# One-hot gate rows by two 1024-column fp16 vector operations per four tokens

## Chip, core and metric

The kernel runs on one core of one Trainium2 chip. The metric is the device time of the whole program in microseconds (us). The core's engines work side by side, each through its own queue in order: TensorE (PE in the profile; its weight loads are listed apart as PEld), VectorE (DVE), ScalarE (ACT), GpSimd (POOL) and SyncE (SP, which only issues transfers here).

## What is computed

One inference step of a decoder layer for 256 prompt tokens and 32 sample tokens: a norm, one input projection, a gated convolution branch, a windowed attention branch, their gated sum, and then PEER, a retrieval over 128 x 128 experts of one neuron each. The change touches only PEER, and there only the prompt tokens:

```python
def body(hc):
    qh = (hc @ wq).reshape(PEER_CHUNK, PEER_HEADS, 2, PEER_HALF)
    s1 = jnp.einsum('chd,hnd->chn', qh[:, :, 0], k1)
    s2 = jnp.einsum('chd,hnd->chn', qh[:, :, 1], k2)
    v1, i1 = lax.top_k(s1, PEER_TOPK)
    v2, i2 = lax.top_k(s2, PEER_TOPK)
    ...
    sv, si = lax.top_k(cand, PEER_TOPK)
    eidx = jnp.take_along_axis(cidx, si, axis=-1)
    gate = jax.nn.softmax(sv, axis=-1)
    act = jax.nn.gelu(jnp.einsum('cd,chkd->chk', hc, u_tab[eidx]))
    return jnp.einsum('chk,chkd->cd', gate * act, v_tab[eidx])
```

Each prompt token picks 8 heads x 16 experts, so 128 pairs (i1, i2) with a gate each. The kernel does not gather for the prompt: it multiplies the tokens with all 16384 rows of `u`, weights the result with a dense table of gates that is zero where no expert was picked, and multiplies that with all rows of `v`.

## The kernel before

Weights come in blocks of 128 x 1024 f32 (368 of them, 512 KB each). Every block is split by `split_next` into a rounded part `whi` (ScalarE, line 106) and the remainder `wlo` (VectorE, line 107, or GpSimd for the blocks in `pool_lo`), three blocks ahead of their use, and each product is three passes (lines 125 to 127).

The part of PEER that the change is about is the loop `for i in range(128)` (line 1025), one iteration for each of the 128 blocks of `u`:

- While the top-k of the tokens is not finished, an iteration does a piece of that on VectorE (`topk_some`). When it is finished the temporary pool `tk` is closed, `act1` is opened, and `gates()` begins (line 1032).
- From then on an iteration issues, in this order: `place_new` for gate tiles that are complete (ScalarE), the split of the block two ahead, the multiplication left over from the iteration before (`late`, line 959, VectorE), `place_held` (line 980, VectorE), one step of `gates()` through `gate_some` (now and then two steps, so that the 67 steps end at block 124), and `run_s(i)`: 24 matmuls of 256 columns, then the GELU by ScalarE, in one piece (line 961) for tokens without gates so far and through the tile `ev` (line 958) for tokens that have them.
- A step of `gates()` takes a group `u` of GT = 4 tokens. `hot(u + 2)` makes, two steps ahead, the one-hot rows on VectorE; then TensorE multiplies the rows of group `u` (line 1008, 8 matmuls of 128 columns) into half of a `wide` tile of 8 tokens, which `place_new` and `place_held` read later. 256 tokens are 64 groups.
- `hot(u)`, lines 985 to 994: the 128 picks of a token lie on the 128 partitions. For each token one operation compares a row 0..127 (`iotaR`, fp16) with the pick's i2 (line 990, tile `hot`, 128 columns), and two more compare with i1 and multiply with the gate's fp16 high and low part (line 992, tile `wgt`). That is 12 operations of 128 columns for a group. The indices and gates are per-partition scalars in f32, from `idxT` and `gaT`, which lines 883 to 891 write when the top-k of 128 tokens is finished.
- The rows `hot` are the weights that TensorE loads, the rows `wgt` are streamed.

VectorE takes its operations in the order in which they are issued; so does TensorE. After the loop comes the product with `v` (line 1079).

Of the kernel before, what the change touches and what calls it, by code (L numbers as in the profile page):

```python
# [10 lines left out]
F32 = mybir.dt.float32  # L11
F32R = mybir.dt.float32r
F16 = mybir.dt.float16
# [3 lines left out]
OP = mybir.AluOpType  # L17
AX = mybir.AxisListType

P = 128  # L20
D = 1024
NT = 288
NP = 256
# [17 lines left out]
GT = 4  # L41
# [24 lines left out]
def emit(ctx, tc, a):  # L66
    nc = tc.nc
    V, S, T, G, SY = nc.vector, nc.scalar, nc.tensor, nc.gpsimd, nc.sync
# [50 lines left out]
    def weights(b):  # L119
        split_ahead(b)  # L120
        return halves.pop(b)
# [88 lines left out]
    with ExitStack() as ca:  # L210
        pa = ca.enter_context(tc.tile_pool(name="pa", bufs=1, side="right"))
        with ExitStack() as c1:
# [78 lines left out]
            def proj(b):  # L291
                w = weights(b)
                xH, xL = xin[0]
                clk[0] = b
                o = acc.get()
                for k in range(KT):
                    if k == KT // 2:
                        flow.step()
                    s = slice(k * P, (k + 1) * P)
                    if b:  # L300
                        mm3(o[:, :NT], (w[0][:, s], w[1][:, s]), (xH[:, k, :], xL[:, k, :]), k == 0, k == KT - 1)
                        continue
                    T.matmul(o[:, :NT], w[0][:, s], xH[:, k, :], start=k == 0, stop=False)
                    T.matmul(o[:, :NT], w[0][:, s], xL[:, k, :], start=False, stop=False)
                for k in range(0 if b else KT):
                    s = slice(k * P, (k + 1) * P)
                    T.matmul(o[:, :NT], w[1][:, s], xH[:, k, :], start=False, stop=k == KT - 1)
                return o[:, :NT]
# [197 lines left out]
            for t in range(3):  # L506
                w = P if t < 2 else NS
# [15 lines left out]
            for i in range(12):  # L523
                o = proj(B_Q + i)
                if i == 0:
                    b = bg.get()
                    for t in range(3):
                        w = P if t < 2 else NS
# [124 lines left out]
            for c in range(8):  # L653
                flow.step()
                w = weights(B_AG + 2 * c)
                clk[0] = B_AG + 2 * c
                o = acc.get()
# [9 lines left out]
                e = wk.tile([P, NT], F32, tag="t", name=f"ga{c}", bufs=5)  # L667
# [36 lines left out]
            for c in range(0, 8, 2):  # L704
                flow.step()
                w = weights(B_BG + 5 * (c // 2))
                ybs = []
                for f in range(2):
                    o = acc.get()
# [7 lines left out]
                for f in range(2):  # L717
                    flow.step()
                    gp = proj(B_BG + 5 * (c // 2) + 1 + 2 * f)
                    e = wk.tile([P, NT], F32, tag="t", name=f"gb{c}_{f}", bufs=5)  # L720
# [61 lines left out]
    kp = ctx.enter_context(tc.tile_pool(name="kp", bufs=1))  # L782
# [2 lines left out]
        S.dma_start(h2rep[32 * q:32 * q + 32, :], h2d)  # L785
    eidx = kp.tile([P, 32], I32, name="eidx")
    gateS = kp.tile([P, 32], F32, name="gateS")
    idxT = kp.tile([P, 2, NP], F32, name="idxT")
    gaT = kp.tile([P, 2, NP], F32, name="gaT")
    iotaR = kp.tile([P, P], F16, name="iotaR")  # L790
    G.dma_start(iotaR, a["iotaR"])
    coh = ExitStack()
    oh = coh.enter_context(tc.tile_pool(name="oh", bufs=1))

    ra = ctx.enter_context(ExitStack())
    pact0 = ra.enter_context(tc.tile_pool(name="pact0", bufs=1, side="right"))
# [2 lines left out]
    tk = ct.enter_context(tc.tile_pool(name="tk", bufs=1, side="right"))  # L799
# [75 lines left out]
    def topk_all():  # L875
        for t in range(2):
            r = [tk.tile([P, 8, TOPK], F32, tag=f"r{i}", name=f"r{t}_{i}", bufs=1) for i in range(3)]
            yield from topk(scores[t], 8, f"tp{t}", r, lambda h: 2 * h + 2 <= scored[0])
            b = bg.get()
            for i in range(3):  # L880
                T.transpose(b[:, i * P:(i + 1) * P], r[i].rearrange("p h k -> p (h k)"), ident)
            yield 0.1
            tt = slice(t * P, (t + 1) * P)
            V.tensor_copy(idxT[:, :, tt], b[:, 0:2 * P].rearrange("p (f c) -> p f c", f=2))
            gs = tk.tile([P, P], F32, tag="gs", name=f"gs{t}", bufs=1)
            V.tensor_scalar_mul(gs, b[:, 2 * P:3 * P], GSCALE)
            bg.put()
            g16 = tk.tile([P, P], F16, tag="g16", name=f"g16_{t}", bufs=1)
            V.tensor_copy(g16, gs)
            V.tensor_copy(gaT[:, 0, tt], g16)  # L890
            V.tensor_sub(gaT[:, 1, tt], gs, g16)
            yield 0.8
        s = tk.tile([P, 16, P], F32, tag="s", name="s_smp", bufs=2)
        b = bg.get()
        for jf in range(4):
            for q in range(4):
                T.matmul(b[32 * q:32 * q + 32, jf * P:(jf + 1) * P], qh[:, 4 * q + jf, NP:NT], keys[:, 4 * q + jf, :],
                         start=True, stop=True, tile_position=(0, 32 * q))
        V.tensor_copy(s[:, 0:4, :].rearrange("p a b -> p (a b)"), b)
        bg.put()  # L900
        yield 1.0
        i1s = tk.tile([P, 2, TOPK], F32, name="i1s")
        i2s = tk.tile([P, 2, TOPK], F32, name="i2s")
        yield from topk(s, 2, "ts", (i1s, i2s, gateS.rearrange("p (h k) -> p h k", h=2)), lambda h: True)
        V.scalar_tensor_tensor(i1s, i1s, 128.0, i2s, op0=OP.mult, op1=OP.add)
        V.tensor_copy(eidx.rearrange("p (h k) -> p h k", h=2), i1s)
        yield 0.3
# [4 lines left out]
    def topk_some(x):  # L912
        budget[0] = min(budget[0], 1.0) + x
        while budget[0] > 0 and not done[0]:
            r = next(gen, 0)
            if r == 0:
                done[0] = True
            elif r is None:
                return
            else:  # L920
                budget[0] -= r
# [11 lines left out]
    for j in range(16):  # L933
        w = weights(B_WQ + j)
        o = acc.get()
# [29 lines left out]
    def place_new(u, full):  # L965
        tt = slice(u * 8, u * 8 + 8)
        f = full.rearrange("p (t i) -> p i t", t=8)
        for c in range(2):
            n = min(max(held[0] - 64 * c, 0), 64)
            if n < 64:  # L970
                S.activation(act[c][:, n:, tt], f[:, 64 * c + n:64 * c + 64, :], AF.Copy, scale=1.0 / GSCALE)
# [11 lines left out]

    def gates():
        def hot(u):
            e = oh.tile([P, GT, P], F16, tag="hot", name=f"hot{u}", bufs=3)
            w = oh.tile([P, GT, 2, P], F16, tag="wgt", name=f"wgt{u}", bufs=3)
            for j in range(GT):
                t = u * GT + j
                V.tensor_scalar(e[:, j, :], iotaR, idxT[:, 1, t:t + 1], None, op0=OP.is_equal)  # L990
                for i in range(2):
                    V.tensor_scalar(w[:, j, i, :], iotaR, idxT[:, 0, t:t + 1], gaT[:, i, t:t + 1],  # L992
                                    op0=OP.is_equal, op1=OP.mult)
            return e, w

        n = NP // GT
        made = {}
        for u in range(-2, n):
            if u + 2 < n:
                made[u + 2] = hot(u + 2)  # L1000
            if u >= 0:
                if u % 2 == 0:
                    full = wide.get()
                e, w = made.pop(u)
                for j in range(GT):
                    jj = (u % 2) * GT + j
                    for i in range(2):
                        T.matmul(full[:, jj * P:(jj + 1) * P], e[:, j, :], w[:, j, i, :], start=i == 0, stop=i == 1)
                if u % 2:
                    placing.append((u // 2, full))  # L1010
            yield
        yield

    placing = []
    gg, first = None, [None]

    def gate_some(i):
        n = 3 + NP // GT
        while stepped[0] < min(n, (i - first[0]) * n / (124 - first[0])):
            assert next(gg, 1) is None  # L1020
            stepped[0] += 1
# [3 lines left out]
    for i in range(128):  # L1025
        if not done[0]:
            topk_some(1.6 if i % 2 else 2.4)
        elif gg is None:
            ct.close()
            pact1 = ra.enter_context(tc.tile_pool(name="pact1", bufs=1, side="right"))  # L1030
            act[1] = pact1.tile([P, 64, NP], F32, name="act1")
            gg, first[0] = gates(), i
        for x in placing:
            place_new(*x)
        split_ahead(B_U + i)
        for f in late:
            f()
        late.clear()
        for x in placing:
            place_held(*x)  # L1040
        placing.clear()
        if gg is not None:
            gate_some(i)
        run_s(i)
        copy_some(1 if i % 4 == 0 else 0)
# [73 lines left out]
    for i in range(V_END):  # L1119
# [14 lines left out]
        if i == 121:  # L1134
            for n in range(2):
                b = bg.get()
# [46 lines left out]
def host(inp):  # L1183
    f = {k: np.ascontiguousarray(np.asarray(v)) for k, v in inp.items()}
    d = {}
# [25 lines left out]
    for g, nm in enumerate(("cache_kv_w128", "cache_kv_w512", "cache_kv_w2048")):  # L1211
        c = f[nm][0]
        d[f"cache{g}"] = c.reshape(8, c.shape[1], D)
        if g == 2:
            c = c[:, rows2]
# [13 lines left out]
    con[:, 160:176] = np.arange(16, dtype=np.float32)[None]  # L1229
    con[:, 176] = EPS  # L1230
    d["consts"] = con
    d["iotaR"] = np.ascontiguousarray(np.broadcast_to(np.arange(P)[None, :], (P, P))).astype(np.float16)

    def dist_mask(dq, win, dil):
        ok = (dq >= 0) & (dq <= win) & (dq % dil == 0)
# [2 lines left out]
    q = np.arange(P)[:, None]  # L1238
# [6 lines left out]
    b4, sl, tt = (x.reshape(-1)[:, None] for x in np.meshgrid(np.arange(4), np.arange(8), np.arange(4), indexing="ij"))  # L1245
# [48 lines left out]
```

## Time and profile before

| | us |
|---|---|
| median of three runs (1338.0 to 1339.51) | 1339.17 |
| the profiled execution: its own time | 1339.22 |
| the profiled execution: span from first to last instruction | 1337.4 |
| TensorE busy in the span | 1277.6 |
| VectorE busy in the span | 1009.7 |
| ScalarE busy in the span | 585.5 |

The page of the profile gives busy time by engine and by slices of the span, the chain of work that ended last, and the groups of instructions by line. The trace behind it can be asked for stretches of time: busy time of each engine in a window, the instructions of one engine in order of time, and groups by line in a window. In an ordered list a row has the start in us, the duration in us, the engine, the line, the operation, what it writes and reads, and the count of instructions merged into it; in brackets stands the idle time of the engine before it and what the profile names as its end. Durations of successive instructions of one engine overlap, because they are pipelined: what an instruction costs in a row of others is the distance from its start to the next start.

### The profile page before, as it was taken

The page shows a single profiled execution, that of the slowest core. Times are in us where ns is not written, and L with a number is a line of the kernel's source. Part 1 is how long each engine was busy: PE and PEld are TensorE (multiplying, and loading weights), DVE is VectorE, ACT ScalarE, POOL GpSimd, SP SyncE. Part 2 cuts the span into 40 slices and gives each one's busy share as a digit, 9 for nine tenths or more (in the row PEclk, how much of TensorE's full clock was granted, in tenths as well). Part 3 has the DMA queues.
Part 4 walks back from the last instruction along what each step waited for, and adds up shares of the span by engine and source line. Part 5 has one row for each costly group of instructions (what it writes and reads, how often), then busy time and mean ns, then how long its engine had stood idle before and what let it go on. Part 6 is the DMA issues. An engine that isn't in the chain of part 4 may idle for free.

```text
span 1337.4 us, 23676 instructions
## 1 busy us (share of the span) xinstructions
PE 1277.6 (96%) x9132; PEld 1140.0 (85%) x9132; DVE 1009.7 (75%) x2348; ACT 585.5 (44%) x971; POOL 182.2 (14%) x122
## 2 busy tenths in 40 slices
PE   6999999999999899999999998999999999999995
PEld 6998998888998899899998887888888888888873
DVE  5736276673593458999989999999868878787874
ACT  4334443433462445445344333333445555555542
POOL 4000000000250133444000000000001111111100
PEclk7999999999999899999999998999999999999998
DMA  7586766655586678677765555555678888888874
GB/s 279 193 314 256 245 236 229 226 207 205 166 258 218 237 250 285 235 270 265 265 232 198 189 189 174 189 189 178 219 283 297 308 297 308 306 303 291 314 277 145
DMA packets 68065, 325.15 MB, mean 243 GB/s; under 512 B 8576, under 2 KB 8736, under 8 KB 59120
## 3 DMA queue, kind: packets, MB, share of 16 engines
q1 hardware_dynamic: 55744, 249.46, 53.6%
q0 software_dynamic: 9760, 67.15, 13.1%
q10 hardware_dynamic: 2448, 7.03, 1.5%
q8 instruction: 72, 1.18, 0.4%
q14 instruction: 41, 0.34, 0.1%
HBM read 317.50 MB, written 60.24 MB: 282 GB/s over the span
## 4 chain that ended last, share of the span: by engine, by line
PE 68%; DVE 25%; DMA 3%; ACT 2%; issue 2%; SPq 0%; DVEq 0%; ACTq 0%; POOLq 0%
PE wide L1079 24%; PE acc L125 12%; PE acc L126 11%; PE acc L127 11%; DVE wgt L992 8%; DVE wlo L107 7%; DVE hot L990 3%; PE bg L760 3%; DVE act L980 2%; DMA raw<-wpack 2%; PE bg L380 1%; PE bg L349 1%; PE bg L468 1%; PE bg L414 1%; ACT whi L106 1%
## 5 line engine op out<-in xcount | busy, mean ns | idle before, releaser
L107 DVE TENSOR_TENSOR wlo<-raw,whi 128x1024 fp32r<-128x1024 f32 x327 | 406.4, 1244 | 223.7 <-ACT whi L106 222.2
L106 ACT CAST whi<-raw 128x1024 fp32r<-128x1024 f32 x360 | 378.1, 1050 | 193.2 <-PE wide L1079 158.3
L125 PE MATMUL acc<-h2H,whi 128*128 128x256 f32 (+1 forms) x1152 | 331.9, 288 | 0.0
L127 PE MATMUL acc<-h2H,wlo 128*128 128x256 f32 (+1 forms) x1152 | 327.3, 284 | 4.3 <-DVE wlo L107 4.0
L126 PE MATMUL acc<-h2L,whi 128*128 128x256 f32 (+1 forms) x1152 | 329.3, 286 | 0.1
L125 PEld LDWEIGHTS acc<-h2H,whi 128*128 128x128 f32 x1152 | 220.0, 191 | 11.3 <-ACT act L961 5.5
L127 PEld LDWEIGHTS acc<-h2H,wlo 128*128 128x128 f32 x1152 | 218.0, 189 | 4.9 <-DVE wlo L107 4.4
L126 PEld LDWEIGHTS acc<-h2L,whi 128*128 128x128 f32 x1152 | 219.5, 190 | 0.4 <-DVE h2L L191 0.4
L125 PE MATMUL acc<-hH,whi 128*128 128x288 f32 x512 | 157.7, 308 | 3.3 <-ACT yb L714 2.4
L1079 PE MATMUL wide<-whi,ah 128*128 128x512 f32 x504 | 155.5, 390 | 1.6 <-ACT ah L1066 1.6
L1079 PE MATMUL wide<-whi,al 128*128 128x512 f32 x504 | 155.2, 389 | 0.0
L1079 PE MATMUL wide<-wlo,ah 128*128 128x512 f32 x504 | 155.2, 389 | 0.0
L127 PE MATMUL acc<-hH,wlo 128*128 128x288 f32 x512 | 150.8, 294 | 1.0 <-DVE wlo L107 1.0
L126 PE MATMUL acc<-hL,whi 128*128 128x288 f32 x512 | 151.1, 295 | 0.0
L992 DVE TENSOR_SCALAR wgt<-iotaR,idxT,gaT 128x128 f16<-128x128 f16 x512 | 133.5, 298 | 0.0
L1079 PEld LDWEIGHTS wide<-whi,ah 128*128 128x128 f32 x504 | 94.4, 188 | 22.2 <-ACT ah L1066 2.7
L1079 PEld LDWEIGHTS wide<-wlo,ah 128*128 128x128 f32 x504 | 94.6, 188 | 19.7
L1079 PEld LDWEIGHTS wide<-whi,al 128*128 128x128 f32 x504 | 94.6, 188 | 19.6
L125 PEld LDWEIGHTS acc<-hH,whi 128*128 128x128 f32 x512 | 96.0, 188 | 15.6 <-issue 8.5
L107 POOL TENSOR_TENSOR wlo<-raw,whi 128x1024 fp32r<-128x1024 f32 x33 | 84.1, 2550 | 121.8 <-ACT whi L106 121.8
L127 PEld LDWEIGHTS acc<-hH,wlo 128*128 128x128 f32 x512 | 96.3, 188 | 1.2 <-DVE wlo L107 1.2
L126 PEld LDWEIGHTS acc<-hL,whi 128*128 128x128 f32 x512 | 96.3, 188 | 0.0
(317 smaller groups left out, 1630.6 us busy)
## 6 DMA issues: line engine op xcount, KB each, us to landing
raw<-wpack SPq DMA_DIRECT2D x368, 512.0 KB
kvs<-cache SPq DMA_DIRECT2D x32, 1020.0 KB
kvs<-cache SPq DMA_DIRECT2D x16, 1016.0 KB
kv<-kc POOLq DMA_DIRECT2D x14, 1024.0 KB, 7.3
kv<-vc POOLq DMA_DIRECT2D x14, 1024.0 KB, 6.1
kvs<-cache SPq DMA_DIRECT2D x8, 496.0 KB
kT_out<-kT ACTq DMA_DIRECT2D x1, 1728.0 KB
v_out<-vn ACTq DMA_DIRECT2D x6, 256.0 KB
```

The lines of the kernel that those rows point to most:

```text
L106: S.copy(hi, raw)
L107: (G if i in pool_lo else V).tensor_sub(lo, raw, hi.bitcast(F32))
L125: T.matmul(out, wh, xh, start=first, stop=False)
L126: T.matmul(out, wh, xl, start=False, stop=False)
L127: T.matmul(out, wl, xh, start=False, stop=last)
L349: T.matmul(dst, qT[rows, g * 4 + pr, t * P:(t + 1) * P], kT[rows, g * 4 + pr, 0:w], start=True, stop=True)
L380: T.matmul(o[rows, :P], vn[:, kb, g * 512 + s * HD:g * 512 + (s + 1) * HD], pt[:, j, :], start=j == 0, stop=j == nb - 1)
L760: T.matmul(o, x, wo[k][m][:, nn], start=k == 0 and i == 0, stop=k == KT - 1 and i == 2)
L980: V.scalar_tensor_tensor(sl, f[:, 64 * c:64 * c + n, :], 1.0 / GSCALE, sl, op0=OP.mult, op1=OP.mult)
L990: V.tensor_scalar(e[:, j, :], iotaR, idxT[:, 1, t:t + 1], None, op0=OP.is_equal)
L992: V.tensor_scalar(w[:, j, i, :], iotaR, idxT[:, 0, t:t + 1], gaT[:, i, t:t + 1], op0=OP.is_equal, op1=OP.mult)
L1079: T.matmul(vacc[t][:, nn], x[:, tt], w[:, nn], start=i == 0 and j == 0, stop=i == 127 and j == 2)
```

## The change

`hot(u)` makes the rows of a group with two operations in place of twelve. Both tiles become 1024 columns of fp16. The first operation (`tensor_tensor`, is_equal) compares `iotaR` with both indices of the four tokens at once; its tile holds the one-hot rows of i1 (f = 0) and of i2 (f = 1). The second (`tensor_tensor`, mult) multiplies the rows of i1 with the high and with the low part of the gate; it reads what the first wrote. Indices and gates are no longer scalars but columns that are repeated 128 times. Tokens are interleaved in pairs, so that the innermost run of each operand is two neighbouring fp16 elements, one of each token; `iotaR` holds each number twice for this. The matmuls therefore read every second column of the tiles, for the weights and for the streamed rows. `idxT` and `gaT` become fp16 and are laid out by groups; the separate copy `g16` is gone. The pool `oh` (tiles `hot`, `wgt`, `ev`) is opened where `gates()` begins, and no longer before the top-k.

```diff
--- before.py
+++ after.py
@@ -785,12 +785,10 @@
         S.dma_start(h2rep[32 * q:32 * q + 32, :], h2d)
     eidx = kp.tile([P, 32], I32, name="eidx")
     gateS = kp.tile([P, 32], F32, name="gateS")
-    idxT = kp.tile([P, 2, NP], F32, name="idxT")
-    gaT = kp.tile([P, 2, NP], F32, name="gaT")
-    iotaR = kp.tile([P, P], F16, name="iotaR")
-    G.dma_start(iotaR, a["iotaR"])
-    coh = ExitStack()
-    oh = coh.enter_context(tc.tile_pool(name="oh", bufs=1))
+    idxT = kp.tile([P, NP // GT, 2, GT], F16, name="idxT")
+    gaT = kp.tile([P, NP // GT, 2, GT], F16, name="gaT")
+    iotaR = kp.tile([P, P, 2], F16, name="iotaR")
+    G.dma_start(iotaR.rearrange("p a b -> p (a b)"), a["iotaR"])
 
     ra = ctx.enter_context(ExitStack())
     pact0 = ra.enter_context(tc.tile_pool(name="pact0", bufs=1, side="right"))
@@ -880,15 +878,14 @@
             for i in range(3):
                 T.transpose(b[:, i * P:(i + 1) * P], r[i].rearrange("p h k -> p (h k)"), ident)
             yield 0.1
-            tt = slice(t * P, (t + 1) * P)
-            V.tensor_copy(idxT[:, :, tt], b[:, 0:2 * P].rearrange("p (f c) -> p f c", f=2))
+            uu = slice(t * P // GT, (t + 1) * P // GT)
+            V.tensor_copy(idxT[:, uu], b[:, 0:2 * P].rearrange("p (f u c) -> p u f c", f=2, c=GT))
             gs = tk.tile([P, P], F32, tag="gs", name=f"gs{t}", bufs=1)
             V.tensor_scalar_mul(gs, b[:, 2 * P:3 * P], GSCALE)
             bg.put()
-            g16 = tk.tile([P, P], F16, tag="g16", name=f"g16_{t}", bufs=1)
-            V.tensor_copy(g16, gs)
-            V.tensor_copy(gaT[:, 0, tt], g16)
-            V.tensor_sub(gaT[:, 1, tt], gs, g16)
+            gs = gs.rearrange("p (u c) -> p u c", c=GT)
+            V.tensor_copy(gaT[:, uu, 0, :], gs)
+            V.tensor_sub(gaT[:, uu, 1, :], gs, gaT[:, uu, 0, :])
             yield 0.8
         s = tk.tile([P, 16, P], F32, tag="s", name="s_smp", bufs=2)
         b = bg.get()
@@ -983,14 +980,14 @@
 
     def gates():
         def hot(u):
-            e = oh.tile([P, GT, P], F16, tag="hot", name=f"hot{u}", bufs=3)
-            w = oh.tile([P, GT, 2, P], F16, tag="wgt", name=f"wgt{u}", bufs=3)
-            for j in range(GT):
-                t = u * GT + j
-                V.tensor_scalar(e[:, j, :], iotaR, idxT[:, 1, t:t + 1], None, op0=OP.is_equal)
-                for i in range(2):
-                    V.tensor_scalar(w[:, j, i, :], iotaR, idxT[:, 0, t:t + 1], gaT[:, i, t:t + 1],
-                                    op0=OP.is_equal, op1=OP.mult)
+            e = oh.tile([P, 2, 2, P, 2], F16, tag="hot", name=f"hot{u}", bufs=3)
+            w = oh.tile([P, 2, 2, P, 2], F16, tag="wgt", name=f"wgt{u}", bufs=3)
+            sh = [P, 4, P, 2]
+            V.tensor_tensor(e.rearrange("p f q i t -> p (f q) i t"), iotaR[:, None].broadcast_to(sh),
+                            idxT[:, u].rearrange("p f (q o t) -> p (f q) o t", o=1, t=2).broadcast_to(sh), op=OP.is_equal)
+            sh = [P, 2, 2, P, 2]
+            V.tensor_tensor(w, e[:, 0:1].broadcast_to(sh),
+                            gaT[:, u].rearrange("p f (q o t) -> p f q o t", o=1, t=2).broadcast_to(sh), op=OP.mult)
             return e, w
 
         n = NP // GT
@@ -1005,13 +1002,14 @@
                 for j in range(GT):
                     jj = (u % 2) * GT + j
                     for i in range(2):
-                        T.matmul(full[:, jj * P:(jj + 1) * P], e[:, j, :], w[:, j, i, :], start=i == 0, stop=i == 1)
+                        T.matmul(full[:, jj * P:(jj + 1) * P], e[:, 1, j // 2, :, j % 2], w[:, i, j // 2, :, j % 2],
+                                 start=i == 0, stop=i == 1)
                 if u % 2:
                     placing.append((u // 2, full))
             yield
         yield
 
-    placing = []
+    placing, coh = [], ExitStack()
     gg, first = None, [None]
 
     def gate_some(i):
@@ -1029,6 +1027,7 @@
             ct.close()
             pact1 = ra.enter_context(tc.tile_pool(name="pact1", bufs=1, side="right"))
             act[1] = pact1.tile([P, 64, NP], F32, name="act1")
+            oh = coh.enter_context(tc.tile_pool(name="oh", bufs=1))
             gg, first[0] = gates(), i
         for x in placing:
             place_new(*x)
@@ -1229,7 +1228,8 @@
     con[:, 160:176] = np.arange(16, dtype=np.float32)[None]
     con[:, 176] = EPS
     d["consts"] = con
-    d["iotaR"] = np.ascontiguousarray(np.broadcast_to(np.arange(P)[None, :], (P, P))).astype(np.float16)
+    d["iotaR"] = np.ascontiguousarray(np.broadcast_to(np.arange(P)[None, :, None], (P, P, 2))).reshape(P, -1).astype(
+        np.float16)
 
     def dist_mask(dq, win, dil):
         ok = (dq >= 0) & (dq <= win) & (dq % dil == 0)
```

## Rows read from the trace of the kernel before

**Rows 1.** The page: its first line, and busy time by engine.
```profile
span 1337.4 us, 23676 instructions
...
PE 1277.6 (96%) x9132; PEld 1140.0 (85%) x9132; DVE 1009.7 (75%) x2348; ACT 585.5 (44%) x971; POOL 182.2 (14%) x122
```

**Rows 2.** Windows: PE, PEld, DVE, ACT, POOL busy (instructions), granted clock, DMA share, GB/s.
```profile
655.00:680.00 25.00, 25.00 (x213) 25.00 (x212) 22.63 (x62) 14.61 (x21) 0.00 (x0) 1.00 0.88 299
...
687.00:951.00 264.00, 248.09 (x2002) 217.92 (x2001) 263.29 (x947) 95.10 (x218) 0.00 (x0) 0.99 0.54 187
```

**Rows 3.** The chain that ended last within 687 to 951 us, shares by line.
```profile
by line: DVE wgt L992 40.1%; DVE wlo L107 25.8%; DVE hot L990 13.1%; DVE act L980 10.2%; DVE act L959 4.1%; issue 3.4%; PE acc L125 1.0%; PE acc L126 0.9%; PE acc L127 0.8%; PE wide L1008 0.6%; ACT whi L106 0.4%; ACT act L971 0.1%
```

**Rows 4.** Groups by line, 687 to 951 us: count, busy us, mean ns, idle before.
```profile
L992 DVE TENSOR_SCALAR wgt<-iotaR,idxT,gaT 128x128 f16<-128x128 f16 x512 | 133.5, 298 | 0.0
...
L126 PEld LDWEIGHTS acc<-h2L,whi 128*128 128x128 f32 x496 | 94.9, 191 | 0.0
...
L990 DVE TENSOR_SCALAR hot<-iotaR,idxT 128x128 f16<-128x128 f16 x256 | 60.8, 237 | 0.0
L1008 PEld LDWEIGHTS <-hot 128*128 128x128 f16 x512 | 36.0, 97 | 35.4 <-DVE hot L990 15.5 <-DVE wgt L992 2.7 <-DVE act L980 1.0
```

**Rows 5.** VectorE in order of time: the first of twelve operations, and what follows them.
```profile
708.68 0.23 DVE L990 TENSOR_SCALAR hot<-iotaR,idxT 128x128 f16<-128x128 f16 x1
...
711.12 1.21 DVE L107 TENSOR_TENSOR wlo<-raw,whi 128x1024 fp32r<-128x1024 f32 x1
```

**Rows 6.** VectorE in order of time: two iterations near the end of the stretch.
```profile
938.24 1.21 DVE L107 TENSOR_TENSOR wlo<-raw,whi 128x1024 fp32r<-128x1024 f32 x1
...
944.70 0.23 DVE L990 TENSOR_SCALAR hot<-iotaR,idxT 128x128 f16<-128x128 f16 x1
...
947.13 1.21 DVE L107 TENSOR_TENSOR wlo<-raw,whi 128x1024 fp32r<-128x1024 f32 x1
```

**Rows 7.** VectorE in the top-k: 1024-column and 512-column f32 operations, the second reading the first.
```profile
558.93 1.23 DVE L863 TENSOR_TENSOR tp_eq<-tp_eq,tp_ixf 128x1024 f32<-128x1024 f32 x1
560.19 1.22 DVE L866 TENSOR_REDUCE r<-tp_eq 128x64 f32<-128x1024 f32 x1
561.33 0.28 DVE L869 TENSOR_REDUCE tp_l<-tp_ex 128x8 f32<-128x128 f32 x1
...
676.47 0.69 DVE L863 TENSOR_TENSOR ts_eq<-ts_eq,ts_ixf 128x512 f32<-128x512 f32 x1
677.19 0.69 DVE L866 TENSOR_REDUCE i2s<-ts_eq 128x32 f32<-128x512 f32 x1
677.80 1.22 DVE L107 TENSOR_TENSOR wlo<-raw,whi 128x1024 fp32r<-128x1024 f32 x1
```

**Rows 8.** Weight loads in order of time: gate loads that found their rows ready.
```profile
692.49 0.45 PEld L1008 LDWEIGHTS <-hot 128*128 128x128 f16 x8
692.90 0.19 PEld L125 LDWEIGHTS acc<-h2H,whi 128*128 128x128 f32 x1
...
714.28 0.50 PEld L1008 LDWEIGHTS <-hot 128*128 128x128 f16 x8
714.98 0.19 PEld L125 LDWEIGHTS acc<-h2H,whi 128*128 128x128 f32 x1 [0.20 <-ACT act L961]
...
717.94 0.58 PEld L1008 LDWEIGHTS <-hot 128*128 128x128 f16 x6
```

**Rows 9.** ScalarE in order of time: evictions of the first and the last blocks with gates.
```profile
699.40 0.18 ACT L958 ACTIVATE ev<-acc 128x8 f32<-128x8 f32 x1 [1.50 <-PE acc L127]
...
954.42 0.38 ACT L958 ACTIVATE ev<-acc 128x248 f32<-128x248 f32 x1 [2.48 <-PE acc L127]
...
965.72 0.38 ACT L958 ACTIVATE ev<-acc 128x256 f32<-128x256 f32 x1 [1.50 <-issue]
```

**Rows 10.** The tile `acc`, 687 to 967 us: count, ns min/median/max, first and last start.
```profile
L958 ACT ACTIVATE ev<-acc x65: 177/284/384, 699.4 to 965.7; 128x256 f32<-128x256 f32 x4, 128x8 f32<-128x8 f32 x2, 128x16 f32<-128x16 f32 x2, 128x24 f32<-128x24 f32 x2
```

**Rows 11.** Line 125 on the weight queue, 687 to 967 us: separate wait instructions.
```profile
L125 PEldq EVENT_SEMAPHORE  x59: 51/51/51, 703.3 to 954.9; - x59
```

## The prediction

> **What bounds the kernel now.** I read the page first: TensorE is busy for 1277.6 of 1337.4 us, VectorE for 1009.7 [rows 1]. That average says TensorE, and it is wrong for the one place that the change touches. The windows show it: at 655 to 680 us, before the gates, TensorE and its loads fill the window and VectorE has room (22.63 of 25); from 687 to 951 us VectorE is busy for 263.29 of 264 us and the loads for only 217.92 [rows 2]. The chain of waits confined to that stretch puts 93% on VectorE, 53% on the lines 990 and 992 that the change replaces [rows 3], and the groups by line show TensorE's gate loads idle 35.4 us in front of them, most of it until `hot` or `wgt` [rows 4]. So time taken from VectorE here is time taken from the program, until TensorE is the later one.
>
> How much room is there? The evictions by line 958 come once for each block, 65 of them [rows 10], from 699.40 to 965.72 us [rows 9]: 64 steps in 266.3 us, 4.16 us each. What TensorE needs for such a step is seen where the rows of a group were ready: gate loads begin at 714.28, the block's own at 714.98, the next gate loads at 717.94 [rows 8], so 0.70 + 2.96 = 3.66 us.
>
> **Part by part.** *The twelve operations that go.* From the first start at 708.68 to the next other work at 711.12 they take 2.44 us [rows 5]; at the end of the stretch it is 2.43 (944.70 to 947.13) [rows 6]. They have no idle time in front of them [rows 4]. I use distances of starts, since the mean durations (237 and 298 ns [rows 4]) overlap: 4 x 237 + 8 x 298 = 3.33 us would count too much.
>
> *The two operations that come.* No operation of the trace has two fp16 tensors and an fp16 result, so I bound the pair by two f32 chains in which the second operation reads the first, as here. At full length, 1024 columns, one column per step: 558.93 to 560.19 to 561.33, so 1.26 + 1.14 = 2.40 us. At half length, 512 columns, which is what 1024 columns cost if two go through at a time: 676.47 to 677.19 to 677.80, so 0.72 + 0.61 = 1.33 us [rows 7]. I take 1.33, because the operands are 16-bit, and the layout gives each of them neighbours of two in the innermost run; 2.40 is the other end and is kept as a rival. Both operations come with no GpSimd work beside them (0.00 in the stretch [rows 2]).
>
> The row shows about 0.20 us for each small operation (2.44 / 12), so most of what goes is cost per instruction. [...]
>
> *VectorE's sum.* It saves 2.44 - 1.33 = 1.11 us per group. 61 of the 64 groups fall between the two evictions (three precede the first). 266.3 - 61 x 1.11 = 199 us would be VectorE's end. The tightest place is the end of the stretch, where `late` and `place_held` are longest: two iterations take 947.13 - 938.24 = 8.89 us [rows 6], less 2 x 1.11 is 6.67, or 3.34 per iteration, still under TensorE's 3.66. VectorE would no longer be last.
>
> *What is late next: TensorE.* 60 steps with a gate group at 3.66 us, the last four without one as they are (965.72 - 954.42 = 11.3 us [rows 9]), and one step with a second group, which adds 0.41 us for 8 loads in a row (692.49 to 692.90 [rows 8]): 219.6 + 11.3 + 0.4 = 231.3 us. Gain: 266.3 - 231.3 = 35.0 us.
>
> In these 3.66 us stands a 0.20 us gap in front of the block's first load [rows 8], with a wait instruction of its own on 59 blocks [rows 11]. At 692.90 there is none. I leave it in, as the waits of that load do not change by the diff; should it go, that is another 59 x 0.20 = 11.8 us.
>
> *The matmuls* keep count and shape, but read every second fp16 column. Lower bound: no change, 0.057 us per load and matmul when ready ((0.50 - 0.097) / 7 [rows 4, 8]). Upper bound: the f32 load's 191 ns in full, unhidden [rows 4]. I take no change: the step between columns becomes four bytes, which is the step of every f32 load and stream of the same loop, whose 24 loads of a block with their matmuls take 2.96 us, about 0.12 for 256 columns. [...] The two ends stay as rivals.
>
> *Waits, order and small things.* The second operation waits for the first; behind it in VectorE's queue stands only the next iteration's split, and rows are made two groups ahead, so TensorE does not wait for this. The wait is inside the 1.33. Opening the pool `oh` where the gates begin adds a wait on the last users of `tk`; these are VectorE's own operations and are over before line 990 first runs, so nothing. The edits in the top-k drop one copy of 128 columns per 128 tokens and are at 0, under work of TensorE; without that cover they are worth two operations, less than 1 us. `iotaR` grows from 32 to 64 KB on GpSimd's queue, far ahead of its use: 0. The transfers must speed up from 4.16 to 3.66 us per block: the share of 0.54 at 187 GB/s becomes some 0.62, and 655 to 680 us ran at 0.88 with TensorE full [rows 2].
>
> The profiled execution took 1339.2 us, 1.8 more than its span and 0.05 from the median of the runs. 1339.2 - 35.0 gives **1304 us**.
>
> **The rivals.** *Loads or streams cost more for the step of two, but hidden in part.* If each pair of load and matmul takes the load's whole 97 ns [rows 4] in place of 57, that is 0.04 x 8 x 61 = 19.5 us: 1324. Against it stands the f32 work above. [...] No row before shows an fp16 step of two.
>
> *Only one of the two operations runs two columns at a time.* The pair is 1.26 + 0.61 = 1.87 us [rows 7]; VectorE ends at 266.3 - 61 x 0.57 = 231.5 us, level with TensorE. Two engines that are late in turn lose some microseconds: about 1309.
>
> *Neither does; the change doesn't do what it says.* The pair is 2.40 us, VectorE stays the bound and saves 61 x 0.04 = 2.4 us: 1337, and within 1334 to 1342 as the real pair is some 0.05 us shorter or longer than the f32 one. For it: innermost runs of only two, and indices repeated with a step of zero between them. [...]
>
> *Slower: the strided weight load is no longer hidden.* If each gate load takes the f32 load's 191 ns [rows 4] and holds its matmul up, a pair costs 0.134 us more, 61 x 8 x 0.134 = 65 us, all on TensorE, which is then the bound: 1369. It turns the sign once a pair costs 35.0 / (61 x 8) = 0.072 us more, that is 0.129 us in all. For it: the weights were contiguous so far, and the f16 load is half as long as the f32 one (97 against 191 ns), so it has something to lose. Against it: f32 loads of 191 ns run hidden at one per 0.12 us in the same blocks.
>
> **How the numbers follow.** Forecast 0.66 (its own range 1292 to 1314: the gap of 0.20 us gone below; above, some ten microseconds of waits between two engines of 3.34 and 3.66 us per step). Load partly dearer 0.11, one operation slow 0.08, both slow 0.08, load unhidden 0.07. The range 1291 to 1326 takes in the first three (0.85) and leaves out what of them lies outside, and the last two. A measurement of this kernel can tell 0.2%, 2.7 us, from no change. Faster by more: the first three and a sixth of the fourth, 0.86; the same: most of the fourth, 0.06; slower: the unhidden load and the rest of the fourth, 0.08.
>
> **What would show it.** In the profile of the changed kernel: each new operation at about 0.69 us (1.22 would be the slow rival); VectorE under 95% busy in the stretch of the gates, with idle time until `whi`; evictions of line 958 3.6 to 3.7 us apart, with no wait of gate loads for `hot`; gate loads at 97 ns and 8 of them in 0.4 to 0.5 us (more is the load rival); the product with `v` unchanged in length but about 35 us earlier. The forecast is wrong if TensorE's loads still wait for VectorE, or if the 3.66 us grow.

## The result, and the profile after

The changed kernel takes 1288.45 us (median; 1286.99 to 1289.37) against 1339.34 us before: a ratio of 0.9621, with a 95% interval of 0.9604 to 0.9638. That is 50.9 us less. The forecast was 1304 us. The direction was right, and so was the engine that is last now (TensorE); one term of the sum, TensorE's step, was too long. The gain was half as large again as forecast, and the time lies 2.5 us under the range. One execution of the last run below (one_step_again), at a mean granted clock of 0.653 where all others have 0.98 to 0.99, took 1732.96 us and is left out of the numbers.

The page of the changed kernel: its first line, busy time by engine, and the chain that ended last by line.

```profile
span 1286.7 us, 22976 instructions
...
PE 1238.5 (96%) x9132; PEld 1128.4 (88%) x9132; DVE 938.9 (73%) x1706; ACT 585.5 (46%) x971; POOL 181.2 (14%) x122
...
PE wide L1078 25%; PE acc L125 16%; PE acc L126 16%; PE acc L127 15%; PE bg L760 3%; PE wide L1005 2%; DVE wlo L107 2%; DMA raw<-wpack 2%; PE bg L380 1%; PE bg L349 1%; PE bg L468 1%; PE bg L414 1%; ACT whi L106 1%; DVE tp_eq L858 1%; PE bg L370 1%
```

The lines moved by a few: `hot` is now made in line 986, `wgt` in 989, the gate matmuls are in 1005, `ev` is in 955. No VectorE line of the gate rows is among the lines with 1% or more of the chain. Where it is confined to 687 to 905 us (to compare with [rows 3], where VectorE had 93%), it reads:

```profile
by line: PE acc L125 28.2%; PE acc L126 27.1%; PE acc L127 26.6%; PE wide L1005 14.0%; DVE wlo L107 1.1%; ACT whi L106 0.9%; DVE act L977 0.8%; DVE wgt L989 0.6%; DVE hot L986 0.3%; ACT act L968 0.3%; DVE act L956 0.2%; issue 0.1%
```

Windows of the stretch (busy us of PE, PEld, DVE, ACT, POOL, then granted clock, DMA share, GB/s), answering [rows 2]:

```profile
700.00:725.00 25.00, 25.00 (x241) 24.61 (x241) 21.06 (x37) 11.83 (x27) 0.00 (x0) 1.00 0.68 234
...
775.00:800.00 25.00, 23.36 (x226) 22.85 (x225) 21.73 (x37) 10.93 (x25) 0.00 (x0) 1.00 0.65 233
...
875.00:900.00 25.00, 25.00 (x238) 24.65 (x236) 24.64 (x38) 10.17 (x25) 0.00 (x0) 1.00 0.65 227
```

TensorE and its loads now fill the windows, but for two in the middle (the one shown, and 24.20 us of 25 from 800 to 825). VectorE has room at the start and hardly any at the end.

The new operations, and the evictions of blocks with gates (count, ns min/median/max, first and last start), answering [rows 4] and [rows 10]:

```profile
L986 DVE TENSOR_TENSOR hot<-iotaR,idxT x64: 677/682/689, 685.8 to 897.0; 128x1024 f16<-128x1024 f16 x64
L989 DVE TENSOR_TENSOR wgt<-hot,gaT x64: 691/692/694, 686.5 to 897.8; 128x1024 f16<-128x1024 f16 x64
...
L955 ACT ACTIVATE ev<-acc x65: 178/284/387, 697.6 to 915.1; 128x256 f32<-128x256 f32 x4, 128x8 f32<-128x8 f32 x2, 128x16 f32<-128x16 f32 x2, 128x24 f32<-128x24 f32 x2
```

The 64 steps between the first and the last eviction took 266.3 us before and take 217.5 now: 48.8 of the 50.7 us by which the span became shorter. Another 1.8 us had been gained by the first eviction (699.4 against 697.6), of which 0.7 us stand in the trace before the top-k begins, where the two programs do the same. This part is not the change's to claim: a second profile of the changed kernel (after_again, below) has its first eviction at 699.1 and its last at 915.0, so 215.9 us in the stretch. Two executions of one kernel differ by some 1.5 us in either part. From the last eviction to the end it is 371.7 us before and 371.6 now.

The weight loads in order of time, answering [rows 8], and the separate wait instructions of line 125, answering [rows 11]:

```profile
714.31 0.46 PEld L1005 LDWEIGHTS <-hot 128*128 128x128 f16 x8
714.73 0.19 PEld L125 LDWEIGHTS acc<-h2H,whi 128*128 128x128 f32 x1
...
717.69 0.46 PEld L1005 LDWEIGHTS <-hot 128*128 128x128 f16 x8
...
L125 PEldq EVENT_SEMAPHORE  x59: 51/51/51, 699.6 to 904.2; - x59
```

A step is 3.38 us (714.31 to 717.69): 0.42 for the gates and 2.96 for the block. The 0.20 us gap in front of the block's first load is gone, and the 59 wait instructions are still there. The new operations in order of time, for their price:

```profile
860.41 0.68 DVE L986 TENSOR_TENSOR hot<-iotaR,idxT 128x1024 f16<-128x1024 f16 x1
861.13 0.69 DVE L989 TENSOR_TENSOR wgt<-hot,gaT 128x1024 f16<-128x1024 f16 x1
861.74 1.22 DVE L107 TENSOR_TENSOR wlo<-raw,whi 128x1024 fp32r<-128x1024 f32 x1
```

### The profile page after: what moved, and what is told of

Read it like the earlier page. It is cut to its first block, busy times and chain, and to the rows that moved or that the text cites. A ratio compares the mean times of both kernels' runs of the same rounds, so it can differ in the third digit from the quotient of the medians.

```text
span 1286.7 us, 22976 instructions
## 1 busy us (share of the span) xinstructions
PE 1238.5 (96%) x9132; PEld 1128.4 (88%) x9132; DVE 938.9 (73%) x1706; ACT 585.5 (46%) x971; POOL 181.2 (14%) x122
## 4 chain that ended last, share of the span: by engine, by line
PE 86%; DVE 7%; DMA 3%; ACT 2%; issue 1%; SPq 0%; DVEq 0%; ACTq 0%; POOLq 0%
PE wide L1078 25%; PE acc L125 16%; PE acc L126 16%; PE acc L127 15%; PE bg L760 3%; PE wide L1005 2%; DVE wlo L107 2%; DMA raw<-wpack 2%; PE bg L380 1%; PE bg L349 1%; PE bg L468 1%; PE bg L414 1%; ACT whi L106 1%; DVE tp_eq L858 1%; PE bg L370 1%
## 5 line engine op out<-in xcount | busy, mean ns | idle before, releaser
L1089 POOL DMA_INDIRECT gt<-uv,eidx x32 | 49.4, 1542 | 255.1 <-DVE accS L1098 254.5
```

Of the source, the lines that this page charges most:

```text
L1089: G.indirect_dma_start(out=gt, out_offset=None, in_=a["uv"], in_offset=bass.IndirectOffsetOnAxis(ap=eidx[:, j:j + 1], axis=0))
```

## The experiments

The theory after the result: in the kernel before, the 0.70 us between the gate loads and the block's own load was not TensorE's need. VectorE was still making those rows. VectorE in order of time in the kernel before, at the place of [rows 8]:

```profile
714.17 0.24 DVE L990 TENSOR_SCALAR hot<-iotaR,idxT 128x128 f16<-128x128 f16 x1
714.34 0.52 DVE L992 TENSOR_SCALAR wgt<-iotaR,idxT,gaT 128x128 f16<-128x128 f16 x2
714.78 1.21 DVE L107 TENSOR_TENSOR wlo<-raw,whi 128x1024 fp32r<-128x1024 f32 x1
```

The gate loads begin at 714.28, while the rows of the last token are made from 714.17 on; they are finished as the next operation takes over at 714.78, and the block's load follows at 714.98, 0.20 us later. The same distance is seen at the neighbouring groups (703.15 and 703.35, 706.80 and 707.00). The rows are issued two groups ahead, but this lead was used up by the fifth group (its loads begin at 702.55, its rows are made until 703.15), since VectorE was the slower one. Rivals: the gap was the price of the wait instruction (W), the new layout is faster for TensorE (L), or the place of the pool is part of the gain.

**The pool alone.** The kernel before with the pool opened later:

```diff
-    coh = ExitStack()
-    oh = coh.enter_context(tc.tile_pool(name="oh", bufs=1))
...
+    placing, coh = [], ExitStack()
...
+            oh = coh.enter_context(tc.tile_pool(name="oh", bufs=1))
             gg, first[0] = gates(), i
```

> The kernel before with one part of the change alone: the pool of the gate rows is opened where the gates begin. Theory: nothing moves, 1339 us, since the first row is made 7 us after the last operation of the top-k; evictions of line 958 stay 4.16 us apart. Rival (the place of the pool is part of the gain): faster by more than 2.7 us.

Measured: 1338.56 us, ratio 0.9994 (0.9984 to 1.0005); evictions from 699.2 to 964.8 us, 4.15 us apart. The place of the pool is worth nothing that the interval tells.

**Half of the rows, everything else as before.**

```diff
-            for j in range(GT):
+            for j in range(GT // 2):
...
-   T.matmul(..., e[:, j, :], w[:, j, i, :], ...)
+   T.matmul(..., e[:, j % 2, :], w[:, j % 2, i, :], ...)
```

> The kernel before with half of the row work left out: rows are made for two of the four tokens of a group (6 operations, 1.22 us in place of 2.44), and the matmuls of the other two tokens read the same rows. Weights and streams stay contiguous, and each block's first load keeps its wait instruction. Theory (in the kernel before, TensorE's 0.70 us at a group and the 0.20 us gap in it were VectorE, which was still making those rows; TensorE itself needs 2.96 + 0.42 = 3.38 us per step): VectorE comes to 2.94 us per step, the gap goes, evictions 3.38 us apart, 1286 to 1290 us. Rival W (the gap is the price of the wait instruction, and went because twelve waits became two): the gap stays, 3.6 to 3.66 us, 1302 to 1306. Rival L (the new layout or the two-operation form makes TensorE's side faster): 8 gate loads stay at 0.50 us or more, 1294 or more.

Measured: 1286.76 us, ratio 0.9601 (0.9582 to 0.9619). Its weight loads in order of time, its wait instructions, its evictions, and a window (columns as above):

```profile
714.25 0.45 PEld L1008 LDWEIGHTS <-hot 128*128 128x128 f16 x8
714.66 0.19 PEld L125 LDWEIGHTS acc<-h2H,whi 128*128 128x128 f32 x1
...
717.59 0.45 PEld L1008 LDWEIGHTS <-hot 128*128 128x128 f16 x8
...
L125 PEldq EVENT_SEMAPHORE  x59: 51/51/51, 699.7 to 902.6; - x59
...
L958 ACT ACTIVATE ev<-acc x65: 177/284/384, 697.7 to 913.4; 128x256 f32<-128x256 f32 x4, 128x8 f32<-128x8 f32 x2, 128x16 f32<-128x16 f32 x2, 128x24 f32<-128x24 f32 x2
...
690.00:900.00 210.00, 208.24 (x1985) 204.79 (x1984) 187.21 (x553) 94.57 (x216) 0.00 (x0) 1.00 0.65 230
```

With the old small operations, the old contiguous layout and the same 59 wait instructions the step is 3.34 us here (3.37 on the mean of the 64 evictions) and there is no gap: 0.41 us from the gate loads to the block's load. So neither the wait instruction nor the layout had cost the 0.28 us (0.70 less 0.42), and the whole gain is got by giving VectorE less to do. W and L fall.

**Two operations without the pairs.** Tokens one after the other; in the innermost run one index is read 128 times:

```diff
-   e = oh.tile([P, 2, 2, P, 2], F16, ...)
+   e = oh.tile([P, 2, GT, P], F16, ...)
-   V.tensor_tensor(e "p (f q) i t", iotaR[:, None], idxT[:, u] "p (f q) o t", is_equal)
+   V.tensor_tensor(e "p (f c) i", iotaR[:, None], idxT[:, u] "p (f c) o", is_equal)
```

(and the same for the product, for `iotaR`, which is 128 columns again, and for the matmuls' columns.)

> The changed kernel without the pairs: still two operations of 1024 fp16 columns per group, but tokens lie one after the other, so that in the innermost run one index (or gate) is read 128 times. TensorE reads contiguous columns. Theory: one column per step for both, about 1.22 us each, 2.40 us the pair; VectorE bounds again, evictions 4.1 us apart, 1335 us within 4, and the 0.20 us gap at the first load is back. Rival (two columns at a time whatever the innermost run, the pairs are not needed): 1286 to 1289 us.

Measured: 1339.14 us, ratio 0.9998 (0.9987 to 1.0009). Its two operations, its evictions, a window, and two weight loads in order of time:

```profile
L986 DVE TENSOR_TENSOR hot<-iotaR,idxT x64: 1211/1217/1223, 686.9 to 947.0; 128x1024 f16<-128x1024 f16 x64
L989 DVE TENSOR_TENSOR wgt<-hot,gaT x64: 1224/1225/1228, 688.1 to 948.3; 128x1024 f16<-128x1024 f16 x64
...
L955 ACT ACTIVATE ev<-acc x65: 177/284/384, 699.6 to 964.4; 128x256 f32<-128x256 f32 x4, 128x8 f32<-128x8 f32 x2, 128x16 f32<-128x16 f32 x2, 128x24 f32<-128x24 f32 x2
...
690.00:900.00 210.00, 180.17 (x1630) 172.63 (x1629) 206.46 (x249) 77.36 (x174) 0.00 (x0) 0.98 0.53 185
...
718.79 0.45 PEld L1005 LDWEIGHTS <-hot 128*128 128x128 f16 x8 [1.02 <-DVE wgt L989]
719.20 0.19 PEld L125 LDWEIGHTS acc<-h2H,whi 128*128 128x128 f32 x1
```

The instruction count is that of the changed kernel, 12 become 2, VectorE is the busy engine again (206.46 of 210 us), and nothing is gained: the whole of the gain hangs on the pairs. The time lies at the upper end of what was expected. One part of the expectation failed: the gap of 0.20 us did not come back. With all rows of a group finished at once, TensorE waits in front of the first gate load (1.02 us) and then runs through (0.41 us from the gate loads to the block's load). The gap of the kernel before belonged to rows that arrive one by one, the last of them while the group's loads were already running.

**Dense columns for TensorE.** The changed kernel, read contiguously:

```diff
-   T.matmul(..., e[:, 1, j // 2, :, j % 2], w[:, i, j // 2, :, j % 2], ...)
+   T.matmul(..., ef[:, 1, j * P:(j + 1) * P], wf[:, i, j * P:(j + 1) * P], ...)
```

> The changed kernel with TensorE reading 128 neighbouring columns for weights and stream in place of every second one; VectorE's work is unchanged (what is multiplied are then columns of two tokens mixed, so the gates are other ones). Theory: the step of two costs nothing, gate loads 97 ns, 8 in 0.42 us, 1288 us within 1.5. Rival (the step costs something that was paid unseen): faster by 2 us or more, loads shorter or closer together.

Measured: 1287.9 us, ratio 0.9609 (0.9591 to 0.9627). Its weight loads in order of time:

```profile
714.81 0.45 PEld L1006 LDWEIGHTS <-hot 128*128 128x128 f16 x8
715.22 0.19 PEld L125 LDWEIGHTS acc<-h2H,whi 128*128 128x128 f32 x1
...
718.18 0.45 PEld L1006 LDWEIGHTS <-hot 128*128 128x128 f16 x8
```

The eight loads take 0.41 us as against 0.42 with every second column, one load 98 ns against 97. Reading every second column costs at most 0.01 us a group here, 0.6 us in all, which no interval tells.

**The second operation twice.**

```diff
+   V.tensor_tensor(w, e[:, 0:1].broadcast_to(sh), gaT[:, u] ..., op=OP.mult)   # once more
```

> The changed kernel with the second operation of each group issued twice, 0.61 us more on VectorE per group and nothing more on TensorE. Theory: VectorE's end in the stretch was 199 us against TensorE's 217; with 61 x 0.61 = 37 us more it is 236 us, VectorE is last again, evictions 3.68 us apart on the mean, the 0.20 us gap is back, 1304 to 1310 us. Rival (there is more room on VectorE than its rows tell, the operations overlap): under 1296 us.

Measured: 1318.55 us, ratio 0.9854 (0.9835 to 0.9873); evictions from 700.5 to 944.1 us, 3.81 us apart. The rival falls, and the time is above the range that I gave. VectorE in order of time:

```profile
883.02 0.68 DVE L986 TENSOR_TENSOR hot<-iotaR,idxT 128x1024 f16<-128x1024 f16 x1
883.74 0.69 DVE L989 TENSOR_TENSOR wgt<-hot,gaT 128x1024 f16<-128x1024 f16 x1
884.46 0.69 DVE L991 TENSOR_TENSOR wgt<-hot,gaT 128x1024 f16<-128x1024 f16 x1
885.07 1.22 DVE L107 TENSOR_TENSOR wlo<-raw,whi 128x1024 fp32r<-128x1024 f32 x1
```

The operation that another follows on the same tile costs 0.72 us (883.74 to 884.46), the one that the split follows 0.61, so the third adds 0.72 and not 0.61; the three take 2.05. With this price, which I did not have before the run (the expectation has 236 us), the prediction's law gives 199 + 61 x (2.05 - 1.33) = 243 us for VectorE's end, and 243.6 were measured. The gap did not come back here either, for the reason given above.

**The first operation with a step of two.** The same tile, its columns taken token by token:

```diff
-   V.tensor_tensor(e "p (f q) i t", iotaR[:, None], idxT[:, u] "p (f q) o t", is_equal)
+   V.tensor_tensor(e "p (f q) t i", iotaR[:, None] "p g t i", idxT[:, u] "p (f q) t o", is_equal)
```

> The changed kernel with the first operation's columns taken in another order: all 128 numbers of one token, then of the next, so that its innermost run has a step of two elements; the result is the same tile. The second operation is as in the changed kernel. Theory (one column per step for the first, two for the second): 1.22 and 0.69 us, the pair 1.87 us, VectorE's end in the stretch 199 + 61 x 0.54 = 232 us against TensorE's 217: VectorE is last again, but by little, about 1303 us. Rival (VectorE's room in the changed kernel swallows it): under 1293 us. Rival (a step of two is dearer than one column per step): over 1310 us.

Measured: 1313.76 us, ratio 0.9812 (0.9794 to 0.9829); evictions from 697.1 to 937.9 us, 240.8 us in all. VectorE in order of time:

```profile
714.91 1.38 DVE L987 TENSOR_TENSOR hot<-iotaR,idxT 128x1024 f16<-128x1024 f16 x1
716.32 0.69 DVE L991 TENSOR_TENSOR wgt<-hot,gaT 128x1024 f16<-128x1024 f16 x1
716.93 1.22 DVE L107 TENSOR_TENSOR wlo<-raw,whi 128x1024 fp32r<-128x1024 f32 x1
```

The first operation takes 1.38 us in place of the 1.22 that I gave it, so the second rival holds: a step of two fp16 elements (1.28 to 1.38 us over the 64 operations) is dearer here than one element read 128 times (1.21 to 1.23 us in no_pairs). The pair is 2.02 us; with it the law gives 199 + 61 x 0.69 = 241 us (232 were expected), and 240.8 were measured.

**One step of the gates per iteration.** The two windows that TensorE doesn't fill have this in them, weight loads of the changed kernel in order of time:

```profile
792.05 0.46 PEld L1005 LDWEIGHTS <-hot 128*128 128x128 f16 x8
794.32 0.46 PEld L1005 LDWEIGHTS <-hot 128*128 128x128 f16 x8 [1.81 <-DVE wgt L989]
794.74 0.19 PEld L125 LDWEIGHTS acc<-h2H,whi 128*128 128x128 f32 x1
...
802.03 0.46 PEld L1005 LDWEIGHTS <-hot 128*128 128x128 f16 x8 [1.00 <-DVE act L977]
```

Here an iteration takes two groups: TensorE waits 1.81 us for the second one's rows and, two groups later, 1.00 us for a gate tile that is not yet placed.

```diff
-        while stepped[0] < min(n, (i - first[0]) * n / (124 - first[0])):
+        while stepped[0] < min(n, i - first[0]):
```

> The changed kernel with one step of the gates in each iteration: the pace that put two steps into the first and into one middle iteration becomes one per iteration. Theory: the stall at the double step (1.8 us for rows, 1.0 us for the gate tile, about 3 us with what hangs on it) and the wait for the very first rows (1.3 us) go, 1283 to 1286 us. Rival (the steps that now come two blocks later delay the end of the stretch by as much): 1288 us or more.

Measured: 1286.0 us, ratio 0.9601 (0.9588 to 0.9615). Once more, with the changed kernel beside it on one chip:

> The changed kernel once more, on the same chip as the next one, as the measure for it: 1288 us within 2.

> The changed kernel with one step of the gates in each iteration, once more. Theory: 2 to 5 us under the changed kernel on the same chip, since its profile had TensorE without any idle time in the stretch. Rival (the gain is within what a chip gives): no difference that the intervals tell.

Measured: the changed kernel 1288.38 us, ratio 0.9619 (0.9602 to 0.9635); one step per iteration 1284.25 us, ratio 0.9591 (0.9576 to 0.9605). The difference is 4.1 us in the medians. The two intervals touch (0.9602 to 0.9605), but both hold the spread of the kernel before; the five executions of each on this chip do not overlap (1283.4 to 1285.74 against 1286.26 to 1290.87). The trace shows the cause gone, in the first of the two profiles of this kernel:

```profile
690.00:900.00 210.00, 210.00 (x1991) 206.94 (x1990) 192.02 (x305) 94.31 (x216) 0.00 (x0) 1.00 0.66 231
```

TensorE is busy for 210.00 of 210 us, in both profiles; in the changed kernel it is 207.57 in the same window. This version is the fastest of all here.

The kernel before has the same place. One weight load there, and a window behind it:

```profile
815.84 0.13 PEld L1008 LDWEIGHTS <-hot 128*128 128x128 f16 x2 [2.72 <-DVE wgt L992]
...
817.00:827.00 10.00, 9.16 (x60) 8.51 (x59) 9.29 (x36) 2.25 (x7) 0.00 (x0) 0.73 0.43 162
```

TensorE waited 2.72 us for the second group's rows, and the granted clock was 0.50 from 817 to 820 us, 0.73 on the mean of the window; in the changed kernel it is 1.00 in all windows of the stretch. VectorE was busy for 9.29 of these 10 us, so in the kernel before, where VectorE was last, the window cost 0.7 us at most.

## Why the prediction was right and where it was wrong

*The bound of the kernel before, VectorE at the lines 990 and 992:* right; half_rows takes only half of their work away and gains as much as the change.

*The price of the two operations, 1.33 us:* right. In the changed kernel they start at 860.41 and 861.13, and the next work at 861.74: 1.33 us, as in the f32 chain of half the length. The choice between 1.33 and 2.40 was the one that mattered: no_pairs is the rival "neither does", and it measured 1339.14 us where 1337 was forecast for it. No row of before showed that 16-bit operands with neighbours of two go through two columns at a time, and no run shows columns per step as such, of f32 neither. What the runs showed are times: 0.68 to 0.69 us for 1024 fp16 columns with the pairs, 1.21 to 1.23 without them (no_pairs).

*VectorE's sum, 199 us if it were last:* right as a law. Three kernels that made VectorE last again came out where it puts them once the measured price of their operations is put in: 243 worked out and 243.6 measured (mult_twice), 241 and 240.8 (equal_step2), and for no_pairs with 2.40 us 264 and 264.8. Before the runs the prices of the first two were taken too low. The count of 61 groups is one too high: the rows of four groups, not of three, were made before the first eviction (the fourth's by 698.98, the eviction at 699.40), which makes 199 some 200.

*What is late next, TensorE at 3.66 us per step:* the engine was right, the term was mis-sized, and this is the step that failed. The prediction took the loads at 714.28 [rows 8] as a place "where the rows of a group were ready", and the heading of [rows 8] says the same. They were not: VectorE was still making the last token's rows, and both the slower loads (0.50 in place of 0.45 us) and the gap of 0.20 us were VectorE, the very cost that the change takes away. The group at 692.49, 0.41 us to the block's load, stood in the same rows and was the ready one. With 0.42 us, as measured after the change, the step is 2.96 + 0.42 = 3.38 us, and 60 of them are 16.8 us less. The evictions came 3.40 us apart on the mean, where 3.6 to 3.7 were forecast. The 0.057 us per load and matmul came from the same 0.50; with 0.45 it is 0.050. The profile's label for the gap named ScalarE's line 961; the distance to VectorE's row told the truth.

*"the waits of that load do not change by the diff":* true, 59 before and 59 after, and beside the point: with a wait instruction in front of it the block's load follows the gate loads after 0.41 us (half_rows) and 0.42 (the changed kernel), without one after 0.41 (at 692.49 [rows 8]), so one that is served early costs nothing that these rows tell. As an alternative it was priced at 11.8 us, without the slower loads (another 60 x 0.08 = 4.8 us), so that the range ended 2.5 us above the time.

*The step with two groups, 0.41 us:* it was 0.4 + 1.81 + 1.00 = 3.2 us. Where two steps follow each other no block lies between them, so the second one's rows are wanted a block's time earlier, and the prediction counted TensorE's work alone. The wait of 2.72 us at the same place of the kernel before was there to be read. Together: 231.3 - 16.8 + 2.8 = 217.3 us; 217.5 and, in the second profile, 215.9 were measured, so an agreement to 0.2 us is in part luck.

*Strided reading:* no cost, as taken (0.42 us for eight loads against 0.41); both rivals of it (partly hidden, unhidden) fall with dense_cols.

*Pool, top-k, `iotaR`, transfers:* nothing that the runs tell. The pool had a run of its own; the top-k edits and `iotaR` had none, and the first eviction at 697.6 and 699.1 us in two profiles of the changed kernel, against 699.4 before, leaves room for no more than the spread of one kernel. The transfers went up to a share of 0.66 over the stretch, and the profile lays no wait of a weight load to one: from 687 to 905 us these waits end with VectorE (2.8 us) or with "issue" (0.6 us).

*"most of what goes is cost per instruction":* an estimate of the prediction, from 0.20 us for each small operation. Twelve operations took 2.44 us and two took 1.33; which part of the 2.44 went with the instructions and which with the columns, no run here shows.

## What to carry to other kernels

What the next engine needs must be read where its input lay ready, and a consumer that trails its producer looks busy (here 0.50 us for eight loads in place of 0.45): check with the producer's own rows that it had finished before. Fewer instructions alone were no gain here: twelve operations merged into two took as long (2.39 against 2.44 us, 711.96 to 714.35 in no_pairs) until the innermost run held two neighbouring 16-bit elements in every operand (1.33 us). A lead of two was a lead only while the producer was the faster one (in the kernel before it was used up by the fifth group), and a step that consumed two at once ate it (a wait of 1.81 us in the changed kernel).

## What was not expected of the hardware

A 1024-column fp16 `tensor_tensor` took 0.68 to 0.69 us with innermost runs of only two elements and a step of zero between them, as long as 512 columns of f32 took (0.69 us [rows 7]); with one element read 128 times it took 1.21 to 1.23 us (no_pairs). With an innermost step of two elements it took 1.28 to 1.38 us (equal_step2), more than the 1.22 with neighbours in the result and the first source and one repeated element in the second. Such an operation of 0.68 or 0.69 us took 0.72 us from start to start where the next one read or overwrote its tile, and 0.61 where the split followed, which does neither (883.02, 883.74, 884.46 and 885.07 in mult_twice). TensorE's f16 loads at a step of two took the same as contiguous ones (97 against 98 ns), and eight of them with their matmuls 0.42 against 0.41 us.
